# A two-layer encoder trunk on one core: inputs queued in source order behind early constant products, and a down-projection's late splits taken apart from their loads

## The chip, the cores and the metric

The kernel runs on one core of a Trainium2 chip. The metric is the device time of one execution in microseconds (us). Five engines work side by side, each through its own instructions in their order: TensorE (PE; its weight loads are shown as PEld), VectorE (DVE), ScalarE (ACT), GpSimd (POOL) and SyncE (SP). SP issues nearly all transfers; POOL issues those that add to their target.

## The reference

Input and output are 1024 frames x 1024 channels, float32. Two layers:

```
x = x + even_mixer(rms_norm(x))      # layer 0: stick-breaking attention (8 heads) beside a causal pooling mixer
x = x + conv_ffn(rms_norm(x))
x = x + odd_mixer(rms_norm(x))       # layer 1: gated linear attention, 4 heads
x = x + conv_ffn(rms_norm(x))

def conv_ffn(h, w_up, conv_w, conv_b, w_down):      # hidden width 2816
    u = h @ w_up
    conv = conv_b + sum(conv_w[j] * shifted(u, j) for j in range(3))
    a, g = split(conv, 2)
    return (silu(a) * g) @ w_down
```

## The kernel before, in words

Activations lie transposed, as eight tiles of 128 channels x 1024 frames (`x[0]` to `x[7]`). Each float32 operand of a matmul is split into a high part `hi` and a remainder `lo`: a cast on ACT, a subtraction on DVE. A product is three matmuls (hi x hi, hi x lo, lo x hi). So each weight and each activation has a chain of its own: load (SP), cast (ACT), subtraction (DVE), matmul (PE).

The order on TensorE is that of the source. The other engines are ordered by the scheduler when the kernel is built, within the data's dependences; `tc.manual_schedule` keeps the order of the source for the engines it names, and `tc.issue_after(ins)` puts what is written under it behind an instruction of the same engine. Each engine then runs its list strictly in order: one that waits holds up all behind it. A tile's buffer is reused when its readers are done.

**The start.** `prm` (norm gains and the like) and the eight tiles `xt` of the input are loaded; `Norm.add` splits each, scaled by its gain, into `h_hi` and `h_lo`, and adds its squares to `nacc`. Between the halves of the first tile stand the halves of the first query and key weights (`pq`, `pk`: the loads into `wraw` and `kg`, the casts, and the subtractions on POOL). `start_qk` multiplies the eight tiles with both weights in turn, 12 matmuls of 512 columns per tile, and then sums the squares with eight small f32 matmuls (`stats`, L286). Value weights (`in_wv`) follow, whose products (`values`) fill TensorE while the query and key chain runs. The parameters of the convolution (`prm[:, C_CONV:]`), the counts `cnt` and the pool weights `praw` are loaded early too.

**A down-projection** (`down`, once per layer) is one level of Strassen-Winograd: seven products, each of 11 steps `j`. Six are run in this order: P1, P5, P6, P3, P7, P4; a step is 12 matmuls into four banks. `prep(n, j)`, called three steps ahead (`LEAD`), fetches the step's right operand into `rb` (4 buffers; for P6 and P4 an accumulating transfer on POOL adds a second block), fetches its left operand into `rw` (4 buffers) where there is one, combines it on DVE (P5, P6, P3, P7), and splits both (`split_block`: two casts, two subtractions into `blk`). SP is on manual order here. The seventh product (P2) comes last, four rows `r` of 11 steps each. Its left operands are a row of weights as two loads, 512 KB into `wraw` (one buffer) and 192 KB into `r3` (one buffer; printed `r`), in rows of 512 bytes: `last_left`. Its right operands are the 11 blocks B21, 256 KB each: `last_right`, two to a tile `b21`. Both load and split at one call, the rows 0 and 1 within P6:

```
            if n == "P6" and j in (2, 6):
                rows[j // 4] = last_left(j // 4)
            k = NJ * (n == "P4") + j - 8
            if n in ("P7", "P4") and k % 2 == 0 and 0 <= k < NJ + 1:
                last_right(range(k, min(k + 2, NJ)))
```

In layer 0 two more loads follow P4's on SP, of the next mixer's key weights (`in_wok`), into `rb` buffers; their split is `kw`.

Of the kernel before, what the change touches and what calls it, by code (L numbers as in the profile page):

```python
# [12 lines left out]
F32 = mybir.dt.float32  # L13
R32 = mybir.dt.float32r
# [43 lines left out]
def trunk_kernel(  # L58
# [35 lines left out]
    def slot(dtype, name):  # L94
        return xpool.tile([P, T], dtype, tag="x", name=name)
# [15 lines left out]


    def load_split(src, pool=None, tags=("whi", "wlo", "wraw"), eng=None, nb=2, raw=None, parts=None,
                   fetched=None):
        srcs = src if isinstance(src, list) else [src]
        n = sum(a.free_size() for a in srcs)
        pool = pool or wpool
        if fetched is not None:
            raw = fetched
        elif raw is None:  # L120
            raw = (pool if len(tags) > 2 else wpool).tile([P, n], F32, tag=tags[2] if len(tags) > 2 else "wraw",
                                                      name="wraw", bufs=2 if "draw" in tags else 1)
# [13 lines left out]
        def part(cs):  # L136
            if fetched is None:
                fetch(cs)
            S.copy(hi[:, cs], raw[:, cs])  # L139
# [111 lines left out]
    class Norm:  # L251
        def __init__(self, gain_col, acc_tile, sq_tile, add_eng=None):
            self.col, self.acc_tile, self.sq_tile = gain_col, acc_tile, sq_tile
            self.h, self.add_eng, self.n = [None] * KT, add_eng, 0

        def add(self, x, parts=None, k=None):
# [11 lines left out]
            if self.n == 1:  # L268
                self.acc = self.acc_tile()
                S.activation(self.acc, x, AF.Square)  # L270
                return
            sq = self.sq_tile()
            S.activation(sq, x, AF.Square)
            (self.add_eng or (V if self.n == KT else G)).tensor_tensor(self.acc, self.acc, sq, op=ALU.add)

# [75 lines left out]
    ones = const.tile([P, P], F32, name="ones")  # L351
    G.memset(ones, 1.0)
    epsc = const.tile([P, 1], F32, name="epsc")
    G.memset(epsc, EPS)
# [49 lines left out]

    def values(half):
        wt = [load_split(wv[half, c], ep if half == 0 else None, ("ath", "atl") if half == 0 else ("whi", "wlo"))
              for c in range(2)]
        for pp in range(2):
# [784 lines left out]
    def split_block(src):  # L1193
        t = hpool.tile([P, T], R32, tag="h", name="blk")
        S.copy(t[:, 0:512], src)  # L1195
        V.tensor_sub(t[:, 512:T], src, t[:, 0:512].bitcast(F32))  # L1196
        return t

    def down(layer, blocks, ready, after, onward):
# [74 lines left out]

        def last_right(js):
            raw = hpool.tile([P, T], R32, tag="h", name="b21").bitcast(F32)
            for cs, j in zip(HALVES, js):
                nc.sync.dma_start(raw[:, cs], blocks[j]["B21"])
                hi = dn.tile([P, 512], R32, tag="ra", name="b21h", bufs=NJ)
                lo = dn.tile([P, 512], R32, tag="rs", name="b21l", bufs=NJ)  # L1280
                S.copy(hi, raw[:, cs])
                V.tensor_sub(lo, raw[:, cs], hi.bitcast(F32))
                b21.append((hi, lo))

        odd = wdn[layer].rearrange("(f two) p k -> two p f k", two=2)[1]

        def last_left(r):
            parts = []
            big = (hpool, ("wraw", "h", "h"), (1, 16, 16)) if r == KT // 2 - 1 else (wpool, ("wraw", "whi", "wlo"), (1, 2, 2))
            for k0, k1, (pool, tags, nb) in ((0, KT, big), (KT, NJ, (dn, ("r3", "r3h", "r3l"), (1, 2, 2)))):  # L1290
                raw, hi, lo = ((wpool if t == "wraw" else pool).tile([P, (k1 - k0) * P], d, tag=t, name=t, bufs=b)
                               for t, d, b in zip(tags, (F32, R32, R32), nb))
                nc.sync.dma_start(raw.rearrange("p (f k) -> p f k", k=P), odd[:, k0:k1, r * P:(r + 1) * P])
                S.copy(hi, raw)
                V.tensor_sub(lo, raw, hi.bitcast(F32))
# [49 lines left out]
        for r in range(half):  # L1345
# [389 lines left out]
```

## Time and profile before

| | |
|---|---|
| median of 3 runs | 2198.51 us (2197.76 to 2200.26) |
| profiled execution | 2199.35 us, span 2197.7 us |
| PE busy in it | 2150.8 us (98%) |
| DVE, ACT, POOL busy | 1664.8 (76%), 1093.1 (50%), 162.1 us (7%) |
| mean DMA traffic | 128 GB/s |
| longest idle of PE | 5.95 us, ahead of its first matmul |

The profiled execution's time lies 1.65 us above its span, which begins with the first and ends with the last recorded instruction. In the rows below, a start or a duration is in us; `[2.08 <-ACT blk L1195]` means that the engine was idle for 2.08 us before the instruction and that the ACT instruction writing `blk` at line 1195 ended that. L153, L155 and L157 are the three matmuls of `mm3`, L1266 those of a down-projection's step.

### The profile page before, as it was taken

To read this page: it belongs to the slowest core of one execution; us is meant where nothing else is said; L and a number is where in the kernel's file an instruction comes from. 1 tells how busy PE (TensorE), PEld (TensorE's weight loads), DVE (VectorE), ACT (ScalarE), POOL (GpSimd) and SP (SyncE) were. 2 spreads that over 40 slices of the span, in tenths; PEclk is the share of its full clock that TensorE was granted. 3 is DMA by queue.
4 is the path that set the end of the run, shared out by engine and by line. 5 is a ranking of instruction groups with operands and counts; after the bars stand their busy time and mean duration, and the time that the engine had idled before them with its cause. 6 is when DMAs were issued, how large, how long until landed. Compare 5 with 4: busy or idle time off the path is not lost.

```text
span 2197.7 us, 28082 instructions
## 1 busy us (share of the span) xinstructions
PE 2150.8 (98%) x10384; PEld 1767.0 (80%) x10384; DVE 1664.8 (76%) x2458; ACT 1093.1 (50%) x1705; POOL 162.1 (7%) x188
## 2 busy tenths in 40 slices
PE   8999989999999999999999999999999999999998
PEld 7889878888878888778887878787788888887776
DVE  5687688698989899777736655557898998987763
ACT  6666566464444444344546362637544444443441
POOL 2240120000000000010000000000000000000110
PEclk9999999999999999999999999999999999999999
DMA  4132332353444434987501111105343444449885
GB/s 152 49 107 87 94 112 94 119 130 106 130 119 126 124 116 124 350 216 233 169 21 40 38 49 38 49 30 145 105 124 116 123 122 120 124 157 327 222 239 157
DMA packets 126201, 280.31 MB, mean 128 GB/s; under 512 B 13408, under 2 KB 27360, under 8 KB 126064
## 3 DMA queue, kind: packets, MB, share of 16 engines
q1 hardware_dynamic: 112528, 251.25, 34.9%
q0 software_dynamic: 13536, 27.27, 7.0%
q8 instruction: 81, 1.33, 0.2%
q14 instruction: 56, 0.46, 0.1%
HBM read 208.21 MB, written 54.53 MB: 120 GB/s over the span
## 4 chain that ended last, share of the span: by engine, by line
PE 61%; DMA 15%; DVE 15%; issue 4%; ACT 4%; SPq 1%; POOL 0%; DVEq 0%; ACTq 0%; POOLq 0%
PE lin L936 10%; PE z L936 7%; PE lin L153 4%; PE lin L155 4%; PE lin L157 4%; DMA rb<-ut 4%; PE t L936 3%; PE d L936 3%; DMA rw<-in_wdn 3%; DVE blk L1196 2%; PE z L157 2%; PE z L153 2%; PE z L155 2%; DMA raw_g<-in_wup 2%; DMA wraw<-in_wup 2%
## 5 line engine op out<-in xcount | busy, mean ns | idle before, releaser
L1038 ACT ACTIVATE c<-u,prm 128x1024 f32<-128x1024 f32 x88 | 109.1, 1244 | 86.7 <-DVE u L964 79.1
L1266 PE MATMUL lin<-blk 128*128 128x512 f32 x396 | 118.6, 400 | 14.0 <-ACT blk L1195 8.6
L1196 DVE TENSOR_TENSOR blk<-rb,blk 128x512 fp32r<-128x512 f32 x124 | 85.1, 686 | 53.9 <-ACT blk L1195 53.4
L153 PE MATMUL lin<-h_hi,whi 128*128 128x512 f32 x288 | 114.2, 432 | 6.6 <-ACT whi L139 6.0
L1039 DVE SCALAR_TENSOR_TENSOR c<-u,prm,c 128x1023 f32<-128x1023 f32 x88 | 112.3, 1278 | 8.5 <-ACT c L1038 8.5
L1195 ACT CAST blk<-rb 128x512 fp32r<-128x512 f32 x124 | 76.6, 618 | 81.2 <-DMA rb<-ut 44.0
L936 PE MATMUL d<-T,a 128*128 128x512 f32 x480 | 115.4, 389 | 0.0
L1041 DVE SCALAR_TENSOR_TENSOR c<-u,prm,c 128x1022 f32<-128x1022 f32 x88 | 112.3, 1276 | 0.0
L1266 PE MATMUL t<-blk 128*128 128x512 f32 x396 | 112.0, 391 | 0.0
L1266 PE MATMUL d<-blk 128*128 128x512 f32 x396 | 111.9, 391 | 0.0
L1266 PE MATMUL z<-blk 128*128 128x512 f32 x396 | 111.6, 390 | 0.0
L964 DVE TENSOR_TENSOR u<-u,rstd_bc 128x512 f32<-128x512 f32 x160 | 107.8, 684 | 0.4
L936 PEld LDWEIGHTS d<-T,a 128*128 128x128 f32 x480 | 90.1, 188 | 18.7
L155 PE MATMUL lin<-h_lo,whi 128*128 128x512 f32 x288 | 104.4, 398 | 0.7 <-DVE h_lo L264 0.7
L1266 PEld LDWEIGHTS lin<-blk 128*128 128x128 f32 x396 | 73.0, 189 | 39.8 <-ACT blk L1195 13.2
L157 PE MATMUL lin<-h_hi,wlo 128*128 128x512 f32 x288 | 104.2, 398 | 0.0
L936 PE MATMUL z<-blk,s34h 128*128 128x512 f32 x320 | 101.3, 398 | 1.4 <-DVE u L995 1.4
L936 PE MATMUL z<-blk,s12h 128*128 128x512 f32 x320 | 100.9, 396 | 0.0
L936 PE MATMUL lin<-T,s34h 128*128 128x512 f32 x320 | 99.5, 392 | 0.8 <-ACT tm L986 0.8
L936 PE MATMUL t<-blk,whi 128*128 128x512 f32 x320 | 99.6, 392 | 0.0
L936 PE MATMUL lin<-blk,whi 128*128 128x512 f32 x320 | 99.5, 392 | 0.0
L936 PE MATMUL lin<-T,s12h 128*128 128x512 f32 x320 | 99.4, 391 | 0.0
(516 smaller groups left out, 6021.0 us busy)
## 6 DMA issues: line engine op xcount, KB each, us to landing
wraw<-in_wup SPq DMA_DIRECT2D x44, 512.0 KB, 3.7
rw<-in_wdn SPq DMA_DIRECT2D x88, 256.0 KB, 4.7
raw_g<-in_wup SPq DMA_DIRECT2D x40, 512.0 KB, 3.8
rb<-ut SPq DMA_DIRECT2D x66, 256.0 KB, 4.4
b<-c SPq DMA_DIRECT2D x22, 512.0 KB, 2.6
ut<-c SPq DMA_DIRECT2D x22, 512.0 KB, 3.8
s<-in_wup SPq DMA_DIRECT2D x40, 256.0 KB, 2.6
s<-s POOLq DMA_DIRECT2D x40, 256.0 KB, 4.4
```

What stands on the lines that cost most here:

```text
L153: PE.matmul(out[i], wh, ah[i], start=first, stop=False)
L155: PE.matmul(out[i], wh, al[i], start=False, stop=False)
L157: PE.matmul(out[i], wl, ah[i], start=False, stop=last)
L936: PE.matmul(ps, w, m, start=first and k == 0 and n == 0, stop=k == 3 and n == 2, skip_group_check=True)
L964: V.tensor_tensor(dst, dst, rstd_bc[:, cs], op=ALU.mult)
L1038: S.activation(c, u, AF.Identity, scale=pcol(b + 2), bias=pcol(b + 3))
L1039: V.scalar_tensor_tensor(c[:, 1:], u[:, :T - 1], pcol(b + 1), c[:, 1:], op0=ALU.mult, op1=ALU.add)
L1041: V.scalar_tensor_tensor(c[:, 2:], u[:, :T - 2], pcol(b), c[:, 2:], op0=ALU.mult, op1=ALU.add)
L1195: S.copy(t[:, 0:512], src)
L1196: V.tensor_sub(t[:, 512:T], src, t[:, 0:512].bitcast(F32))
L1266: PE.matmul(ps, l, m, start=first and j == 0 and i == 0, stop=j == NJ - 1 and i == 2, skip_group_check=True)
```

## The change

Four edits.

1. At the start, 24 f32 products of the constant tile `ones` with itself (`WARM`) go to TensorE ahead of all other matmuls; their result is not read.
2. The input loop puts SP on manual order. The loads of the input tiles stand ahead of all but the first halves of the query and key weights; the second halves follow the second and third tile; the value weights come behind the last tile, and conv parameters, counts and pool weights behind the value weights. The first halves' subtractions go to DVE. The second tile is split by halves too, and each addition to `nacc` stands one tile later.
3. `last_left` and `last_right` load at the call and return `later`, which splits. Row 0 is loaded at step 10 of P6 and split at step 3 of P3, row 1 at step 4 of P3 and split at step 9; the rows 2 and 3 load and split at one call, as before.
4. The B21 loads come two steps earlier (from step 6 of P7); their splits stay where they were. All moved splits are put behind the latest `split_block` (`behind_latest`).

```diff
+    warm = bank("d")
+    for _ in range(WARM):
+        PE.matmul(warm[:, 0:P], ones, ones, start=True, stop=True, skip_group_check=True)
...
+    queue = ExitStack()
+    queue.enter_context(tc.manual_schedule(engines={mybir.EngineType.SP}))
     for k in range(KT):
...
-            pq[1]()
-            pk[1]()
+            norm.first = split_ins[0]
         else:
             nc.sync.dma_start(xt, xT[k * P:(k + 1) * P, :])
-        norm.add(xt, HALVES if k == 0 else None)
-    nc.sync.dma_start(prm[:, C_CONV:], par[:, C_CONV:])
-    nc.sync.dma_start(cntc, cnt)
+            if k < 3:
+                (pq, pk)[k - 1][1]()
+        norm.add(xt, HALVES if k < 2 else None)
+    queue.close()
...
-            parts.extend(lambda cs=cs: part(cs) for cs in HALVES)
+            parts.extend(lambda cs=cs, e=e: part(cs, e) for cs, e in zip(HALVES, (V, eng)))
...
-    v0 = values(0)
+    v0 = values(0, value_weights(0))
+    inputs_in = split_ins[1]
+    with tc.issue_after(inputs_in):
+        nc.sync.dma_start(prm[:, C_CONV:], par[:, C_CONV:])
+        nc.sync.dma_start(cntc, cnt)
...
-            parts = []
+            raws = []
             for k0, k1, (pool, tags, nb) in ((0, KT, big), (KT, NJ, (dn, ("r3", "r3h", "r3l"), (1, 2, 2)))):
...
                 nc.sync.dma_start(raw.rearrange("p (f k) -> p f k", k=P), odd[:, k0:k1, r * P:(r + 1) * P])
-                S.copy(hi, raw)
-                V.tensor_sub(lo, raw, hi.bitcast(F32))
-                parts += [(hi[:, sl], lo[:, sl]) for sl in (slice(k * P, (k + 1) * P) for k in range(k1 - k0))]
-            return parts
+                raws.append((raw, pool, tags, nb))
+
+            def later():
+                parts = []
+                for raw, pool, tags, nb in raws:
+                    n = raw.free_size()
+                    hi, lo = (pool.tile([P, n], R32, tag=t, name=t, bufs=b) for t, b in zip(tags[1:], nb[1:]))
+                    S.copy(hi, raw)
+                    V.tensor_sub(lo, raw, hi.bitcast(F32))
...
+                rows[r] = parts
+            return later
...
+        ROWS, LATER = [("P6", 10), ("P3", 4)], [("P3", 3), ("P3", 9)]
...
-            if n == "P6" and j in (2, 6):
-                rows[j // 4] = last_left(j // 4)
-            k = NJ * (n == "P4") + j - 8
-            if n in ("P7", "P4") and k % 2 == 0 and 0 <= k < NJ + 1:
-                last_right(range(k, min(k + 2, NJ)))
+            if (n, j) in LATER:
+                with behind_latest():
+                    due.pop(0)()
+            if (n, j) in ROWS:
+                due.append(last_left(ROWS.index((n, j))))
+            k = NJ * (n == "P4") + j - 6
+            if n in ("P7", "P4") and k % 2 == 0 and 0 <= k < NJ + 3:
+                if due:
+                    with behind_latest():
+                        due.pop(0)()
+                if k < NJ + 1:
+                    due.append(last_right(range(k, min(k + 2, NJ))))
```

What SP issues first, before and then after (`xt` are input tiles, `wraw` and `kg` the query and key weights, `in_wv` the value weights; x7 is seven in a row):

```order
L347 DMA prm<-in_par 128x44
L391 DMA xt<-in_xT 128x512
L128 DMA wraw<-in_wqk 128x512
L391 DMA xt<-in_xT 128x512
L128 DMA kg<-in_wqk 128x512
L128 DMA wraw<-in_wqk 128x512
L128 DMA kg<-in_wqk 128x512
L398 DMA prm<-in_par 128x352
L399 DMA cntc<-in_cnt 128x64
L396 DMA xt<-in_xT 128x1024 x7
L570 DMA praw<-in_poolw 128x128 x2
L128 DMA wraw<-in_wv 128x1024
```

```order
L131 DMA kg<-in_wqk 128x512
L417 DMA xt<-in_xT 128x1024
L131 DMA wraw<-in_wqk 128x512
L417 DMA xt<-in_xT 128x1024
L131 DMA kg<-in_wqk 128x512
L417 DMA xt<-in_xT 128x1024 x5
L131 DMA wraw<-in_wv 128x1024 x2
L809 DMA prm<-in_par 128x352
L810 DMA cntc<-in_cnt 128x64
L596 DMA praw<-in_poolw 128x128 x2
```

The first five rows are the same in both; after them the second input tile now stands ahead of two half weights, the conv parameters and the counts.

What SP issues around the rows' loads in layer 0's down-projection, before (`rb<-ut` are right operands of P6) and then after (`rb<-b`, `rw` are P3's, from step 3 on):

```order
L1211 DMA rb<-ut_6253 128x512
L1293 DMA wraw<-in_wdn 128x8x128
L1293 DMA r_8168<-in_wdn 128x3x128
L1211 DMA rb<-ut_6514 128x512
L1211 DMA rb<-ut_6775 128x512
L1211 DMA rb<-ut_7036 128x512
L1211 DMA rb<-ut_7297 128x512
L1293 DMA wraw<-in_wdn 128x8x128
L1293 DMA r_8268<-in_wdn 128x3x128
L1211 DMA rb<-ut_7552 128x512
```

```order
L1338 DMA wraw<-in_wdn 128x8x128
L1338 DMA r_8373<-in_wdn 128x3x128
L1251 DMA rb<-b_5760 128x512
L1251 DMA rw<-in_wdn 128x512
L1251 DMA rb<-b_6021 128x512
L1251 DMA rw<-in_wdn 128x512
L1251 DMA rb<-b_6282 128x512
L1251 DMA rw<-in_wdn 128x512
L1251 DMA rb<-b_6543 128x512
L1251 DMA rw<-in_wdn 128x512
L1251 DMA rb<-b_6804 128x512
L1251 DMA rw<-in_wdn 128x512
```

Behind the last of these rows, step 7 of P3, stand the second row's two loads, and then step 8's `rb` and `rw`.

ACT at the end of P4 in layer 0, from step 9's left cast on, before and then after:

```order
L1195 CAST blk<-rw 128x512
L1195 CAST blk<-rb 128x512
L1195 CAST blk<-rw 128x512
L1195 CAST blk<-rb 128x512
L1281 CAST b21h<-b_9126 128x512
L1341 CAST kw<-rb 128x512 x2
```

```order
L1225 CAST blk<-rw 128x512
L1402 CAST kw<-rb 128x512 x2
L1225 CAST blk<-rb 128x512
L1225 CAST blk<-rw 128x512
L1225 CAST blk<-rb 128x512
L1325 CAST b21h<-b_9110 128x512
```

The two casts of the key weights have moved from behind P4's last split to between step 9's left and right casts.

More of the change, by code (lines that the diff above doesn't have):

```diff
@@ L41 @@
 FGROUP = 2
+WARM = 24
 C_MIXE = 0
@@ L253, in __init__ @@
             self.col, self.acc_tile, self.sq_tile = gain_col, acc_tile, sq_tile
-            self.h, self.add_eng, self.n = [None] * KT, add_eng, 0
+            self.h, self.add_eng, self.n, self.first = [None] * KT, add_eng, 0, None
         def add(self, x, parts=None, k=None):
@@ L269, in add @@
                 self.acc = self.acc_tile()
-                S.activation(self.acc, x, AF.Square)
+                with tc.issue_after(self.first) if self.first is not None else ExitStack():
+                    S.activation(self.acc, x, AF.Square)
                 return
@@ L273, in add, with add_up @@
             S.activation(sq, x, AF.Square)
-            (self.add_eng or (V if self.n == KT else G)).tensor_tensor(self.acc, self.acc, sq, op=ALU.add)
+            def add_up():
+                (self.add_eng or (V if self.n == KT else G)).tensor_tensor(self.acc, self.acc, sq, op=ALU.add)
+            if self.first is None:
+                add_up()
+                return
+            if self.n > 2:
+                with tc.issue_after(b.ins):
+                    self.due()
+            self.due = add_up
+            if self.n == KT:
+                add_up()
         def behind(self):
@@ L392, in trunk_kernel, with value_weights, values @@
                 p[0]()
-            pq[1]()
-            pk[1]()
+            norm.first = split_ins[0]
         else:
             nc.sync.dma_start(xt, xT[k * P:(k + 1) * P, :])
-        norm.add(xt, HALVES if k == 0 else None)
-    nc.sync.dma_start(prm[:, C_CONV:], par[:, C_CONV:])
-    nc.sync.dma_start(cntc, cnt)
+            if k < 3:
+                (pq, pk)[k - 1][1]()
+        norm.add(xt, HALVES if k < 2 else None)
+    queue.close()
     h = norm.h
     vt = [None] * NPAIR
-    def values(half):
-        wt = [load_split(wv[half, c], ep if half == 0 else None, ("ath", "atl") if half == 0 else ("whi", "wlo"))
-              for c in range(2)]
+    def value_weights(half):
+        return [load_split(wv[half, c], ep if half == 0 else None, ("ath", "atl") if half == 0 else ("whi", "wlo"))
+                for c in range(2)]
+    def values(half, wt=None):
+        wt = wt or value_weights(half)
         for pp in range(2):
@@ L778, in start_qk @@
         yield None
-    v0 = values(0)
+    v0 = values(0, value_weights(0))
+    inputs_in = split_ins[1]
+    with tc.issue_after(inputs_in):
+        nc.sync.dma_start(prm[:, C_CONV:], par[:, C_CONV:])
+        nc.sync.dma_start(cntc, cnt)
     fl = Filler()
@@ L1194, in split_block, with behind_latest @@
         t = hpool.tile([P, T], R32, tag="h", name="blk")
-        S.copy(t[:, 0:512], src)
-        V.tensor_sub(t[:, 512:T], src, t[:, 0:512].bitcast(F32))
-        return t
+        a = S.copy(t[:, 0:512], src)
+        b = V.tensor_sub(t[:, 512:T], src, t[:, 0:512].bitcast(F32))
+        latest[:] = a.ins, b.ins
+        return t
+    latest = []
+    def behind_latest():
+        st = ExitStack()
+        for ins in latest:
+            st.enter_context(tc.issue_after(ins))
+        return st
     def down(layer, blocks, ready, after, onward):
@@ L1278, in last_right @@
                 nc.sync.dma_start(raw[:, cs], blocks[j]["B21"])
[L1279 to L1283, printed above, removed]
+            def later():
+                for cs, j in zip(HALVES, js):
+                    hi = dn.tile([P, 512], R32, tag="ra", name="b21h", bufs=NJ)
+                    lo = dn.tile([P, 512], R32, tag="rs", name="b21l", bufs=NJ)
+                    S.copy(hi, raw[:, cs])
+                    V.tensor_sub(lo, raw[:, cs], hi.bitcast(F32))
+                    b21.append((hi, lo))
@@ L1285, in down @@
+            return later
         odd = wdn[layer].rearrange("(f two) p k -> two p f k", two=2)[1]
         def last_left(r):
-            parts = []
             big = (hpool, ("wraw", "h", "h"), (1, 16, 16)) if r == KT // 2 - 1 else (wpool, ("wraw", "whi", "wlo"), (1, 2, 2))
+            raws = []
             for k0, k1, (pool, tags, nb) in ((0, KT, big), (KT, NJ, (dn, ("r3", "r3h", "r3l"), (1, 2, 2)))):
-                raw, hi, lo = ((wpool if t == "wraw" else pool).tile([P, (k1 - k0) * P], d, tag=t, name=t, bufs=b)
-                               for t, d, b in zip(tags, (F32, R32, R32), nb))
+                raw = (wpool if tags[0] == "wraw" else pool).tile([P, (k1 - k0) * P], F32, tag=tags[0], name=tags[0], bufs=1)
@@ L1293, in last_left, with later @@
                 nc.sync.dma_start(raw.rearrange("p (f k) -> p f k", k=P), odd[:, k0:k1, r * P:(r + 1) * P])
-                S.copy(hi, raw)
-                V.tensor_sub(lo, raw, hi.bitcast(F32))
-                parts += [(hi[:, sl], lo[:, sl]) for sl in (slice(k * P, (k + 1) * P) for k in range(k1 - k0))]
-            return parts
+                raws.append((raw, pool, tags, nb))
+            def later():
+                parts = []
[4 more added lines that the diff above has]
+                    V.tensor_sub(lo, raw, hi.bitcast(F32))
+                    parts += [(hi[:, sl], lo[:, sl]) for sl in (slice(k * P, (k + 1) * P) for k in range(n // P))]
+                rows[r] = parts
@@ L1299, in down @@
+            return later
         LEAD = 3
@@ L1305, in down @@
         half = KT // 2
-        rows = {}
+        rows, due = {}, []
+        ROWS, LATER = [("P6", 10), ("P3", 4)], [("P3", 3), ("P3", 9)]
         for i, (n, j) in enumerate(order):
@@ L1350, in down @@
             if r + 2 < half:
-                rows[r + 2] = last_left(r + 2)
+                last_left(r + 2)()
             if r == 0:
```

9 lines of the change are left out of this document (5 added, 4 removed).

## The prediction

> **What bounds the kernel now.** I read the page first, then what TensorE waited for, then the down-projections stage by stage, then the single rows around each edit.
>
> ```profile
> PE 2150.8 (98%) x10384; PEld 1767.0 (80%) x10384; DVE 1664.8 (76%) x2458; ACT 1093.1 (50%) x1705; POOL 162.1 (7%) x188
> ```
>
> TensorE is the bound: 47 us of a 2197.7 us span are all that order can still win, besides half-clock time. Its longest sums of waiting (engine, instruction, releaser: us, times, longest):
>
> ```profile
> PE lin L1266 <- ACT blk L1195: 8.6, 10, 2.1
> PE lin L153 <- ACT whi L139: 6.0, 1, 6.0
> ```
>
> The first lies in the down-projections, the second is the kernel's start; the diff edits just these two places. A pass of a down-projection (P6, P3, P7, P4) is 11 steps of 12 matmuls. Busy time by pass, layer 0 and then layer 1:
>
> ```profile
> 943.80:980.80 37.00, 33.24 (x133) 25.70 (x132) 22.48 (x35) 17.11 (x30) 7.09 (x9) 0.95 0.93 225
> 980.80:1010.70 29.90, 29.90 (x133) 24.77 (x132) 26.10 (x43) 15.90 (x28) 0.00 (x0) 1.00 0.69 223
> 1010.70:1040.70 30.00, 30.00 (x134) 24.82 (x133) 19.34 (x32) 11.11 (x20) 3.77 (x5) 1.00 0.77 238
> 1040.70:1071.30 30.60, 30.38 (x134) 24.68 (x133) 23.42 (x38) 15.29 (x28) 5.74 (x7) 1.00 0.94 260
> 2030.40:2066.50 36.10, 31.63 (x133) 24.54 (x132) 21.25 (x33) 16.19 (x28) 6.92 (x8) 1.00 0.87 214
> 2066.50:2096.50 30.00, 30.00 (x134) 24.82 (x133) 26.31 (x44) 15.80 (x28) 0.00 (x0) 1.00 0.70 226
> ...
> 2126.40:2162.50 36.10, 32.24 (x134) 24.50 (x133) 24.45 (x39) 15.58 (x28) 6.05 (x7) 1.00 0.86 235
> ```
>
> The columns are window, sum, PE, PEld, DVE, ACT, POOL, clock, DMA share, GB/s. A pass that doesn't wait takes 29.9 us: 2.72 us a step, 0.227 us a matmul. P6 loses 7.1 and 6.2 us, P4 0.7 and 6.2. P3 and P7 (layer 1's P7 is left out) lose nothing, but DVE is busy 26 of 30 us in P3.
>
> **The late splits.** The rows of P6 in layer 0 that show the loss:
>
> ```profile
> 954.39 1.05 ACT L1294 CAST whi<-wraw 128x1024 fp32r<-128x1024 f32 x1 [1.59 <-DMA wraw<-in_wdn]
> 970.39 0.50 PE L1266 MATMUL lin<-blk 128*128 128x512 f32 x1 [2.08 <-ACT blk L1195]
> L1295 DVE TENSOR_TENSOR wlo<-wraw,whi 128x1024 fp32r<-128x1024 f32 x2 | 2.5, 1225 | 3.5 <-ACT whi L1294 3.5
> L1295 DVE TENSOR_TENSOR r3l<-r,r3h 128x384 fp32r<-128x384 f32 x2 | 1.1, 551 | 0.0
> ```
>
> ACT stands at a cast whose load has not landed, with the splits of P6 queued behind it. But TensorE's end is not set there alone. Call the splits the feed; its pace is read from the subtractions of step 0 of P6 and step 0 of P3, layer 0 and then layer 1:
>
> ```profile
> 941.22 0.69 DVE L1196 TENSOR_TENSOR blk<-rb,blk 128x512 fp32r<-128x512 f32 x1
> 976.35 0.68 DVE L1196 TENSOR_TENSOR blk<-rb,blk 128x512 fp32r<-128x512 f32 x1
> 2027.70 0.69 DVE L1196 TENSOR_TENSOR blk<-rb,blk 128x512 fp32r<-128x512 f32 x1
> 2064.31 0.68 DVE L1196 TENSOR_TENSOR blk<-rb,blk 128x512 fp32r<-128x512 f32 x1
> ```
>
> That is 35.1 and 36.6 us for 11 steps. The load also slows P6's own transfers. DMA landings from 932 to 945 us (first two lines, ahead of the load) and from 945 to 972:
>
> ```profile
> rb<-ut SPq DMA_DIRECT2D x5, 256.0 KB, 3.3
> rb<-b POOLq DMA_DIRECT2D x3, 256.0 KB, 4.2
> ...
> rb<-b POOLq DMA_DIRECT2D x8, 256.0 KB, 6.2
> rb<-ut SPq DMA_DIRECT2D x6, 256.0 KB, 5.5
> wraw<-in_wdn SPq DMA_DIRECT2D x2, 512.0 KB, 7.8
> ```
>
> One of four `rb` buffers is taken for load, accumulate, cast (1.05 for twice the size: 0.6) and subtraction (0.7): 3.3 + 4.2 + 1.3 = 8.8 us alone, 2.2 us a step, below TensorE's 2.72; 5.5 + 6.2 + 1.3 = 13.0 beside the load, 3.25 a step, above it. With the load and its casts gone P6 should not wait, and its feed takes 11 x 2.2 = 24 us at best; four x additions at its head (2.7 us of DVE) make it 27. The feed is ahead by 8.1 and 9.6 us at P3. What it pays back:
>
> - The second row's load stands on SP behind step 7 of P3, and its buffer is free only after the first row's subtraction, which DVE runs behind step 6's splits; step 8's `rb` and `rw` wait behind it on SP. Step 8's splits come 3.4 us (two x additions and the first row's two subtractions) + L + 2.0 (subtraction, cast, subtraction) after step 6's, where DVE needs 2 x 2.4 now (26.1 us for 11 steps). L is a landing behind 704 KB: between 3.3 (the `rb` row) and 7.8 (the `wraw` row), nearer the first since nothing accumulates there: 5. So 5.6 lost. The steps behind, landed meanwhile, win back some 1.5; the first row's load slows the loads of steps 3 and 4 by about 1. P3 pays 5.1, bounds 3.4 and 7.9. The casts on ACT are covered (16 us of 30 busy).
> - The second row's subtractions (1.23 + 0.55 = 1.8 us) go to the head of P7, where DVE is busy 19 of 30 us: I take half, 0.9.
> - Two of the eleven B21 loads that run beside P4's own now go ahead of them: 5% of 11 x (768 + 256) KB, and of P4's 31 to 36 us some 1 us gained (0 to 1.5). The B21 splits stay in place.
>
> Layer 0: 8.1 - 5.1 - 0.9 + 1.0 = 3.1, bounds -1.6 and 6.2. Layer 1: 4.6 by the same sum; P6's 6.2 is all there is to win, so I take 4.0 between 0 and 6.2. In both layers most of the stall that P6 loses is late again in P4, where TensorE then waits for `rb`: only what the feed gains is kept. SP's queue is otherwise unmoved, POOL's accumulates keep their order.
>
> **The key weights at the end of P4, layer 0 only.** The scheduler now puts both `kw` casts ahead of step 9's `rb` cast on ACT. The rows before (SP's issue, step 9's cast, the second `kw` cast):
>
> ```profile
> 1058.36 5.16 SPq L1211 DMA_DIRECT2D rb<-in_wok  x2
> 1064.41 0.62 ACT L1195 CAST blk<-rb 128x512 fp32r<-128x512 f32 x1 [0.42 <-DMA rb<-ut]
> 1067.81 0.62 ACT L1341 CAST kw<-rb 128x512 fp32r<-128x512 f32 x1 [0.37 <-DMA rb<-in_wok]
> ```
>
> The second load waits for step 8's buffer, so its landing moves with step 8. Step 9's cast goes from 1064.4 to 1067.8 + 0.5, 3.9 us later, and ends at 1068.9. P4 ends at 1071.3 in the table, so step 9 began two steps earlier, at 1065.9: TensorE waits 3.0. A wait of that length has a second price:
>
> ```profile
> 968.90:972.30 3.40, 1.69 (x6) 1.18 (x7) 1.76 (x3) 2.15 (x5) 0.82 (x1) 1.00 1.02 253
> 972.30:975.70 3.40, 3.40 (x10) 2.64 (x9) 3.09 (x5) 2.20 (x5) 0.00 (x0) 0.50 0.91 275
> 2054.30:2057.70 3.40, 1.64 (x8) 1.02 (x6) 1.22 (x1) 1.65 (x3) 0.86 (x1) 1.00 1.09 254
> 2057.70:2061.10 3.40, 3.11 (x13) 2.37 (x14) 3.05 (x6) 2.09 (x5) 0.00 (x0) 1.00 0.97 176
> ```
>
> After a stretch of 3.4 us with PE half idle the clock was 0.50 for the next 3.4 us (1.7 us lost); after another as idle, in layer 1, it was not. At 3.0 us idle I take the dip at 8 in 10: 1.4. Together -4.4, bounds -4.7 and 0. The Trainium skill ("TensorE: Matmul & The Clock Gate", Part 1) has it that the clock is gated after at least one idle window of about 3.4 us; by that there would be no dip and the term would be -3.0. The row at 972 differs, after only 2.1 us of idling, and the row decides.
>
> **The start.**
>
> ```profile
> 0.95 0.21 POOL L352 MEMSET ones<- 128x128 f32 x1
> 5.95 1.58 PE L153 MATMUL lin<-h_hi,whi 128*128 128x512 f32 x2 [5.95 <-ACT whi L139]
> 8.46 1.06 PE L157 MATMUL lin<-h_hi,wlo 128*128 128x512 f32 x2
> 9.31 0.82 PE L153 MATMUL t<-h_hi,whi 128*128 128x512 f32 x2
> 9.97 0.62 PE L155 MATMUL t<-h_lo,whi 128*128 128x512 f32 x2
> 10.46 1.15 ACT L263 ACTIVATE h_hi<-xt,prm 128x1024 fp32r<-128x1024 f32 x1 [1.27 <-DMA xt<-in_xT]
> 31.86 1.84 PE L286 MATMUL d<-ones,nacc 128*128 128x2 f32 x16
> 10.00:20.00 10.00, 8.66 (x37) 6.55 (x36) 8.36 (x8) 9.54 (x10) 1.98 (x2) 1.00 0.92 363
> ```
>
> The first tile runs at half clock (8.46 to 9.31: 0.43 us a matmul; from 9.97 on 0.23); the eight tiles end at 31.86. The 24 products of constants are 48 records (the code's 8 f32 matmuls at L286 are 16) of 1.84/16 = 0.115 us, 0.23 at half clock, and can start at 1.2, when `ones` is set. If half a busy stretch of 3.4 us is enough, as above, the clock rises 1.7 to 5.1 us after that; in the middle, at 4.7, 7.5 of the 24 are done, the other 16.5 take 3.8: they end at 8.5 (7.6 to 9.4). That is later than 5.95, but all 96 real matmuls then run at 0.23: 8.5 + 22.1 = 30.6, gain 1.2. Bounds 0.4 and 1.6, since the data ends it: the second tile, with 0.72 MB less ahead at 363 GB/s, lands 2.0 us sooner and is split at 10.6, 0.7 before its turn. Splits on DVE (0.7 us) in place of POOL (1.3) are covered; the second value load waits for the first one's split, as before, and is used only behind the stats matmuls; conv parameters, counts and pool weights go behind it, and no work of the first 40 us reads them but one cast of pool weights, on ACT, which has gaps there.
>
> By the same section of the Trainium skill, a whole free-running window has to be busy before the clock rises: 3.4 to 6.8 us after the start, so that the products would end between 8.4 and 10.1 and the term be -0.3 to 1.3. The rise before 9.97 for a start at 5.95 fits both, and no other row here tells them apart.
>
> **Sum.** 1.2 + 3.1 - 4.4 + 4.0 = 3.9 us. The profiled execution took 2199.35 (span 2197.7, the rest lies around it): 2195.4. It stands 0.8 above the median of 2198.51, so for a median I say 2194.6.
>
> **Rivals.**
> - The `kw` casts cost nothing, because the feed is ahead at P4's end or the load lands sooner. For: P4 of layer 0 loses only 0.7 now. Against: there TensorE no longer stands 7 us in P6, and the feed is only 3 us sooner. 3.9 + 4.4 = 8.3: 2190.2.
> - All that P6 loses (13.3) is kept and nothing comes back. For: P3 and P7 lose nothing now, with DMA at 0.69 to 0.77. Against: P4 of layer 1 waits already. 14.5: 2184.
> - Slower: the second row's load holds SP for longer than the feed has in hand. Two steps of TensorE are 5.4 us, so it stalls at step 8 of P3 for L + 3.4 + 2.0 - 5.4 = L less what is in hand at step 6. At step 0 of P3 that is 980.8 - 977.0 = 3.8 now, 4.8 by the sum, and more at step 6; it decides when L passes that. With L = 7.8 and 2 in hand (1.5 at step 0 of P3 in layer 1 now) TensorE idles 5.8 with a dip of 1.7, 15.0 in both layers: 15.0 + 4.4 - 13.3 - 1.2 = 4.9 more, 2203.4.
> - It does little: the feed gains nothing, `kw` waits less, the start stays: 2198.
>
> **Chances.** Forecast case (2192 to 2198) 0.42; `kw` free 0.24; all kept 0.09; SP held 0.13; little 0.12. 0.2% is 4.4 us, about what a measurement of this kernel can tell: faster means below 2194.1. Faster 0.24 + 0.09 + 0.17 of the forecast case = 0.50; slower is over half of the SP rival, 0.08; within 0.42. The range leaves out the case of all kept and the slower half of the SP rival: 2187.5 to 2201.
>
> **What would show it.** First real matmul near 8.5 and the stats matmuls near 30.6; P6 near 30 us in both layers; a wait on SP ahead of P3's second `wraw`, and DVE waiting for `rw` of step 8; P4 longer in layer 0, with ACT waiting on `in_wok` and TensorE idle some 3 us, PEclk below 1 after it. Wrong if P3 shows PE idle, if P4 of layer 0 stays at 30.6, or if `kw` doesn't wait.

## The result, and the profile after

| | before | after |
|---|---|---|
| median of 7 runs | 2197.76 us (2193.97 to 2202.03) | 2210.36 us (2203.23 to 2215.10) |
| ratio after / before, with 95% interval | | 1.0052 (1.0039 to 1.0065): some 11 us slower |
| profiled execution, span | 2199.35, 2197.7 | 2210.36, 2208.7 |

The forecast was 2194.6 in a range of 2187.5 to 2201: the sign was wrong. Busy time of the engines after:

```profile
PE 2158.1 (98%) x10432; PEld 1773.3 (80%) x10432; DVE 1667.5 (75%) x2461; ACT 1091.5 (49%) x1706; POOL 160.5 (7%) x186
```

To find where the time went, the two traces' matmuls were matched one by one in TensorE's order; the table gives how much later (plus) or earlier (minus) each kernel's TensorE starts the same matmul than the profiled execution of before, at marks on the clock of before (us). The pass named at a mark is the one that ends there; differences along a row are what each stretch cost. A row is one execution, and not always a typical one: those of e1 and e14 took 4.6 and 6.0 us more than the medians of their kernels. A half-clock stretch, below, is one of 3.4 us in which the granted clock of TensorE was 0.50.

| kernel | 62, start | 423, attention | 940, P5 | 980, P6 | 1010, P3 | 1040, P7 | 1073, P4 | 1519 | 1570 | 2029, P5 | 2066, P6 | 2096, P3 | 2161, P4 |
|---|---|---|---|---|---|---|---|---|---|---|---|---|---|
| after | -0.9 | -5.1 | -4.7 | -10.3 | -4.0 | -4.0 | +4.6 | +4.9 | +10.6 | +9.6 | +4.7 | +9.6 | +11.0 |
| start alone (e1) | -0.2 | -4.6 | -5.8 | -3.5 | -3.5 | -3.5 | +2.2 | +1.3 | +7.9 | +6.9 | +5.2 | +5.2 | +7.4 |
| down alone (e2) | +0.8 | -2.2 | -2.5 | -7.0 | -0.8 | -0.8 | +5.7 | +5.1 | +5.1 | +4.3 | +0.4 | +6.0 | +6.7 |
| rows alone (e3) | +1.3 | -0.8 | -1.9 | -7.5 | -2.2 | -2.2 | +0.8 | +0.8 | +0.8 | +1.0 | -2.5 | +1.9 | -0.7 |
| B21 alone (e4) | +0.3 | -2.8 | -3.3 | -6.3 | -6.3 | -6.3 | +4.7 | +4.2 | +4.2 | +3.0 | +4.9 | +4.9 | +5.8 |
| order of inputs alone (e5) | +1.9 | 0.0 | -0.1 | -1.9 | -1.9 | -1.9 | +2.7 | +2.1 | +2.1 | +2.3 | +0.6 | +0.6 | -0.6 |
| products alone (e6) | +0.2 | -4.6 | -4.4 | -1.9 | -1.5 | -1.5 | +0.8 | +0.8 | +8.3 | +7.1 | +7.4 | +7.4 | +6.6 |
| late second row (e7) | +0.9 | -0.9 | -2.2 | -8.3 | -8.3 | -8.3 | -1.6 | -1.7 | -1.7 | -1.9 | -6.6 | -6.6 | -3.8 |
| 64 products (e14) | +8.3 | +10.2 | +9.4 | +8.2 | +8.2 | +8.2 | +13.8 | +13.7 | +13.7 | +13.1 | +12.1 | +12.1 | +12.3 |

Between 62 and 423 nothing was changed, and the kernels still differ there, from 4.8 us won (e6) to 1.9 lost (e14): half-clock stretches fall there or not (three between 180 and 275 in before, none in after). Only stretches that were edited, or that differ in all kernels with an edit, are read.

**The start** came out at the times that were said (starts and busy time of TensorE, after):

```profile
1.21 7.15 PE L372 MATMUL d<-ones 128*128 128x128 f32 x48 [1.21 <-POOL ones L368]
8.11 0.71 PE L156 MATMUL lin<-h_hi,whi 128*128 128x512 f32 x2
30.83 1.84 PE L302 MATMUL d<-ones,nacc 128*128 128x2 f32 x16
```

The first real matmuls are later than before (5.95) and at full clock, and the sums of squares stand 1.0 us earlier than before (31.86). The experiments put that gain down to the order of the inputs and not to the products: the sums stand at 31.90 with the products alone (e6), at 31.32 and 31.11 with the order alone (e5, e13), and between 31.86 and 33.02 in the eight kernels whose start is the old one.

**The passes**, in the same columns as in the prediction (P6, P3 and P4, layer 0 and then layer 1):

```profile
939.10:970.60 31.50, 30.82 (x134) 24.68 (x133) 17.35 (x28) 13.20 (x24) 7.00 (x9) 1.00 0.93 220
970.60:1006.70 36.10, 32.05 (x133) 25.81 (x133) 26.62 (x43) 16.84 (x30) 0.00 (x0) 0.95 0.62 201
...
1036.60:1075.90 39.30, 32.99 (x134) 25.70 (x133) 25.22 (x41) 16.94 (x30) 6.05 (x7) 0.96 0.78 204
2040.00:2071.20 31.20, 30.77 (x134) 24.64 (x133) 17.50 (x29) 13.20 (x24) 6.92 (x8) 1.00 0.92 220
2071.20:2106.10 34.90, 32.12 (x134) 25.86 (x133) 25.80 (x42) 16.11 (x28) 0.00 (x0) 0.95 0.65 207
...
2136.10:2174.20 38.10, 33.74 (x137) 26.26 (x136) 24.74 (x40) 14.80 (x27) 6.05 (x7) 0.96 0.80 212
```

P6 fell from 37.0 and 36.1 to 31.5 and 31.2. P3, which took 29.9 and 30.0, takes 36.1 and 34.9; P4 of layer 0 takes 39.3 in place of 30.6. The clock column shows a half-clock stretch in P3 and in P4 of both layers. Of the waits of SP's queue between 960 and 1075, in layer 0, these matter here, after and then before (us, times, longest):

```profile
SPq L1338 <- DVE wlo L1347: 9.4, 1, 9.4
SPq L1319 <- DVE b21l L1326: 5.5, 1, 5.5
```

```profile
SPq L1278 <- DVE b21l L1282: 1.7, 2, 1.5
```

The first line is the wait in P3 that the prediction named: the second row's load (L1338) stands on SP until the first row's subtraction (`wlo`) has freed `wraw`. The second is new and was not forecast: a B21 load (L1319) stands 5.5 us for the subtraction of an earlier B21 tile. Both stop TensorE (first two rows: step 8 of P3; third row: step 5 of P4). The fourth row, step 9 of P4, is the wait behind the key weights:

```profile
995.70 0.50 PE L1306 MATMUL lin<-blk 128*128 128x512 f32 x1 [3.14 <-ACT blk L1225]
997.11 0.73 PE L1306 MATMUL lin<-blk 128*128 128x512 f32 x2 [0.91 <-DVE blk L1226]
1054.32 0.49 PE L1306 MATMUL lin<-blk 128*128 128x512 f32 x1 [2.78 <-ACT blk L1225]
1069.90 0.49 PE L1306 MATMUL lin<-blk 128*128 128x512 f32 x1 [2.30 <-ACT blk L1225]
```

In the timeline the B21 wait reads so (SP's issues, the end of the subtraction that it waited for, and the cast behind the late load):

```profile
1034.03 0.43 SPq L1251 DMA_DIRECT2D rw<-in_wdn  x1
1040.00 0.83 SPq L1319 DMA_DIRECT2D b<-b  x2
1041.24 0.32 SPq L1251 DMA_DIRECT2D rb<-ut  x1
```

```profile
1038.69 1.28 DVE L1326 TENSOR_TENSOR b21l<-b,b21h 128x512 fp32r<-128x512 f32 x2
```

```profile
1053.65 0.62 ACT L1225 CAST blk<-rb 128x512 fp32r<-128x512 f32 x1 [6.42 <-DMA rb<-ut]
```

SP stands from 1034.5 to 1040.0, until the subtraction (1038.69 + 1.28) ends. Only then does it issue step 5's `rb` at 1041.24, which lands and is accumulated to by 1053.6. A raw B21 tile (`b21`) is one of the 16 buffers of the tag `h` that all `blk` splits use in turn. Loaded two steps earlier and split where it always was, it holds its buffer longer than the ring takes to come round, so that SP has to wait for the subtraction which frees it.

**The middle** shows a loss in code that no edit touched: between 1519 and 1570, at the end of the odd mixer, after falls 5.7 us behind. There ACT writes the squares `nsq` in turn, and POOL's accumulating transfers add them to `nacc`, each after the one before it has landed. The third and the sixth of the squares, before and then after:

```profile
1524.37 1.04 ACT L332 ACTIVATE nsq<-x 128x1024 f32<-128x1024 f32 x1
...
1540.01 1.06 ACT L332 ACTIVATE nsq<-x 128x1024 f32<-128x1024 f32 x1 [1.75 <-DVE T L918]
```

```profile
1531.45 1.06 ACT L348 ACTIVATE nsq<-x 128x1024 f32<-128x1024 f32 x1 [1.97 <-DMA nacc<-nsq]
...
1549.71 1.06 ACT L348 ACTIVATE nsq<-x 128x1024 f32<-128x1024 f32 x1 [4.16 <-DMA nacc<-nsq]
```

The first two squares stand 5.0 us later in after, as all else does there; the third stands 7.1 later and the sixth 9.7. TensorE in the end waits 2.0 us ahead of the sums of squares, with a half-clock stretch behind it (clock 0.50 from 1564.3 to 1567.7); before it did not wait at that place. Before, and then after:

```profile
1552.86 1.84 PE L286 MATMUL t<-ones,nsq 128*128 128x2 f32 x16
...
1561.76 1.95 PE L302 MATMUL t<-ones,nsq 128*128 128x2 f32 x16 [1.97 <-DVE nsq L357]
```

The transfers of the same 9 us, from the first `xs` load on, before (1515 to 1524) and then after (1520 to 1529); `xs` and the accumulates are issued by SP and POOL (KB each, median us to landing), and q8 is a queue that carries instructions (packets, MB, share):

```profile
xs<-x SPq DMA_DIRECT2D x4, 512.0 KB, 4.2
nacc<-nsq POOLq DMA_DIRECT2D x1, 512.0 KB, 4.6
```

```profile
q8 instruction: 1, 0.02, 1.1%
xs<-x SPq DMA_DIRECT2D x4, 512.0 KB, 6.0
nacc<-nsq POOLq DMA_DIRECT2D x1, 512.0 KB, 7.2
```

Before has no q8 transfer in its 9 us. The only thing added in after is one 16 KB transfer of instructions, and the accumulate takes 2.6 us longer to land. The three accumulates behind it take 5.2, 5.8 and 5.7 us (5.0, 5.0 and 4.6 before), now issued within 0.5 us of an `xs` load; how one small transfer slows the large ones is not shown by the traces. Which engine's instructions these are, the whole page of after tells:

```profile
q8 instruction: 82, 1.34, 0.3%
```

1.34 MB over TensorE's 2 x 10432 instructions (matmuls and weight loads) is 64 bytes each, which fits q8 carrying TensorE's code, 256 instructions to a transfer. The 24 constant products are 48 + 48 instructions: they move every later transfer of code ahead by 96 instructions, some 11 us at 0.227 us for two. In before the transfer falls at 1528.8, in after at 1523.2, which on the clock of before is 1518.3 (transfers from 1528 to 1530 in before, from 1523 to 1525 in after):

```profile
q8 instruction: 1, 0.02, 2.8%
```

```profile
q8 instruction: 1, 0.02, 5.1%
```

### The profile page after: what moved, and what is told of

The parts are those of the page before. It is cut to its first block, busy times and chain, and to the rows that moved or that the text cites. A ratio compares the mean times of both kernels' runs of the same rounds, so it can differ in the third digit from the quotient of the medians.

```text
span 2208.7 us, 28152 instructions
## 1 busy us (share of the span) xinstructions
PE 2158.1 (98%) x10432; PEld 1773.3 (80%) x10432; DVE 1667.5 (75%) x2461; ACT 1091.5 (49%) x1706; POOL 160.5 (7%) x186
## 3 DMA queue, kind: packets, MB, share of 16 engines
q1 hardware_dynamic: 112528, 251.25, 34.9%
q8 instruction: 82, 1.34, 0.3%
```

## The experiments

Two theories stood against one another. The queue theory: the loss is made by two waits on SP in the down-projections. Its rival, or companion: the start costs it, in the middle. Each ratio below is to the kernel before, timed beside it on the same chip, with its 95% interval; 0.001 is 2.2 us.

**e1, edits 1 and 2 alone; e2, edits 3 and 4 alone.**

> Edits 1 and 2 alone (the constant products and the order of the inputs); the down-projections are as before. The trace after lies 0.9 us ahead of the trace before at 90 us, 5.1 at 270 (before has three half-clock stretches between 180 and 275 us that after lacks) and 4.9 behind it again between 1520 and 1565, where nothing was changed. Queue theory (the loss is made in the down-projections by two waits on SP): 0.9 us faster for sure, up to 5 if the half-clock stretches went away because of the start: 2193 to 2198 against 2198, and 1520 to 1565 not late. Rival (the start shifts the whole kernel against its accumulating transfers and costs some 5 us in the middle): 2198 to 2203, with TensorE idle ahead of the sums of squares near 1560.

> Edits 3 and 4 alone (rows split apart from their loads, B21 loads two steps earlier); the start is as before. Queue theory: all of the loss is here: P6 wins 5.7 in both layers, P3 loses 6.3 and 5.1, P4 loses 9.0 (2.3 of it the key weights) and 1.4: +5.4 us, and not less than +2: 2201 to 2210. Rival (the loss is the start's or the middle's): 2195 to 2200.

Measured: e1 1.0013 (0.9999 to 1.0027), e2 1.0039 (1.0024 to 1.0054). Together 1.0052, which is all of after. In its profiled execution e1 loses 6.6 us in the middle, e2 nothing there (table), so the queue theory is not the whole. By its time alone e1 cannot be told from before; e6, below, is what shows the start's price in time.

**e3, edit 3 alone; e4, edit 4 alone.**

```diff
# e3, against after (start as before)
-            k = NJ * (n == "P4") + j - 6
...
+            k = NJ * (n == "P4") + j - 8
+            if n in ("P7", "P4") and k % 2 == 0 and 0 <= k < NJ + 1:
+                last_right(range(k, min(k + 2, NJ)))()
# e4, against after (start as before)
-            if (n, j) in LATER:
...
+            if n == "P6" and j in (2, 6):
+                last_left(j // 4)()
```

> Edit 3 alone: the rows' loads and splits as after, B21 loads and splits at one call as before. Queue theory: P6 wins 11.4 in both layers together, and P3 pays 11.4 because the second row's load holds SP for 9 us behind the first row's subtraction: -3 to +3 us, 2195 to 2201, with PE idle in step 8 of P3 (3 to 4 us and a half-clock stretch) and P4 of layer 0 without the 2.8 us wait at step 5 and without the key weights' wait. Rival (the rows alone carry the loss): 2203 to 2212. Rival of the prediction (P3 pays only 5): 2189 to 2193.

> Edit 4 alone: B21 loads two steps ahead of their splits, rows loaded and split within P6 as before. Queue theory: SP waits some 5 us in both layers for the subtraction of an earlier B21 tile (its buffer), with P4's own loads queued behind it, so TensorE waits 0.8 and 2.8 us at steps 3 and 5 of P4, and 2.3 for the key weights: +4 to +10 us, 2202 to 2208. Rival (earlier B21 loads help or are free, as the prediction took them): 2195 to 2199, or up to 2202 if the key weights alone cost 2.3 to 4.4.

Measured: e3 0.9997 (0.9986 to 1.0007), e4 1.0044 (1.0030 to 1.0059). P3 and P4 of layer 0 in e3:

```profile
973.30:1008.50 35.20, 32.10 (x133) 25.85 (x133) 26.01 (x43) 16.20 (x28) 0.00 (x0) 0.95 0.65 206
...
1038.40:1071.40 33.00, 31.18 (x131) 23.94 (x130) 23.00 (x38) 15.48 (x28) 6.05 (x7) 1.00 0.92 260
```

The rows' edit wins 5.6 and 3.5 us in the two P6, and P3 takes back 5.3 and 4.4. Edit 4 makes the loss in the down-projections. Its wait on SP and P4 of layer 0:

```profile
SPq L1289 <- DVE b21l L1296: 5.3, 1, 5.3
```

```profile
1035.10:1076.70 41.60, 34.42 (x134) 26.65 (x133) 26.07 (x42) 18.01 (x31) 6.04 (x7) 0.92 0.75 194
```

**e5, the order of inputs without products; e6, the products alone.**

> The start's new order of inputs without the constant products (edit 2 alone). Both kernels with the products lose 5.7 and 6.6 us near 1520 to 1565, where a 16 KB transfer of instructions falls at 1519.9 and 1523.2, among the loads and the first accumulate of the norm's sums; in the three traces without the products it falls elsewhere (1528.8 in before) and nothing is lost. Theory (the 96 instructions of the products move where TensorE's code is fetched): the instruction transfer is back near 1529, no idle ahead of the sums of squares near 1556; the first tile runs at half clock again: 2195 to 2199. Rival (the order of inputs, or the drift of transfers, makes the loss in the middle): 2200 to 2205 with the same idle of some 2 us.

> Before with the 24 constant products alone (edit 1). Theory of the moved code fetch: 5 to 6 us lost near 1520 to 1565 as in the other two kernels with the products, 1.2 at most won at the start: 2201 to 2206. Rival (chance, or the order of inputs): no loss there, 2195 to 2199.

Measured: e5 0.9994 (0.9984 to 1.0005), e6 1.0034 (1.0021 to 1.0048). The products alone lose 7.5 us in the middle, the order nothing. e1, which has both, came out 4.6 us below e6, more than the order alone wins (1.3); how much of that is the spread of the intervals, or of executions that do not lose in the middle, is open. e6's transfers over the same 9 us:

```profile
q8 instruction: 1, 0.02, 0.9%
xs<-x SPq DMA_DIRECT2D x4, 512.0 KB, 5.9
nacc<-nsq POOLq DMA_DIRECT2D x1, 512.0 KB, 7.1
```

**e7, the second row's load where SP need not wait; e8, B21 loaded and split at one call, both two steps earlier.**

```diff
# e7, against e3
-        ROWS, LATER = [("P6", 10), ("P3", 4)], [("P3", 3), ("P3", 9)]
+        ROWS, LATER = [("P6", 10), ("P3", 9)], [("P3", 3), ("P7", 3)]
# e8, against before
-            k = NJ * (n == "P4") + j - 8
+            k = NJ * (n == "P4") + j - 6
```

> Edit 3 with the second row's load issued at step 9 of P3 in place of step 4, and split at step 3 of P7; B21 and start as before. Queue theory: by then the first row's subtraction has long been done, SP does not wait for it, and P3 no longer pays its 9.5 (4.4 in layer 1, 5.3 in layer 0 in the trace with edit 3 alone), while P6 keeps its 5.6 and 3.5: 2188 to 2192. Rival (the load itself, not SP's wait, slows P3, and would slow P7 as well): 2195 to 2199. Rival (what P6 wins is late again in P4, which waits for its accumulated operands): 2194 to 2198, with longer waits in P4.

> Before with loads and splits of B21 both two steps earlier (edit 4 without its taking apart). The key weights' casts stand ahead of step 9's last splits here too, so their wait of 2.3 us, with a half-clock stretch at worst, stays. Queue theory (what costs is the buffer that a loaded B21 tile holds until its late split): no wait of 5 us on SP for a B21 subtraction, no 2.9 us wait at step 5 of P4: 2199 to 2203. Rival (the earlier transfers themselves push P4's operands back): 2205 to 2211 with the waits of steps 3 and 5 as in edit 4.

Measured: e7 0.9990 (0.9980 to 1.0001), e8 1.0018 (1.0005 to 1.0031). P3 and P4 of layer 0 in e7:

```profile
972.50:1002.40 29.90, 29.90 (x134) 24.76 (x133) 25.14 (x41) 13.91 (x25) 0.00 (x0) 1.00 0.75 249
...
1033.90:1069.50 35.60, 32.72 (x132) 24.16 (x133) 26.80 (x44) 18.17 (x34) 6.90 (x8) 1.00 0.95 264
```

P3 loses nothing, and neither does P7 up to its last matmul, though the load now runs beside it (the table has -8.3 at 1010 and at 1040). So the load alone is free there, and what P3 paid was SP's wait. But P4 then takes 35.6, and with a wait of 1.3 us ahead of its first matmul it gives back 6.7 and 2.8 us of the two layers' gain: the rival that P6's win is late again in P4 held. In e8 the long wait for a B21 subtraction is gone,

```profile
SPq L1278 <- DVE b21l L1282: 0.3, 1, 0.3
```

and so is more than half of e4's loss: 1.0044 to 1.0018. That is the price of taking the splits apart from the loads, 5.7 us, give or take 4 by the two intervals. The profiled execution of e8, which took 6.2 us more than the median of e8, shows less of it: P4 of layer 0 still takes 39.2 us (41.6 in e4), though no wait of 2.9 us stands at step 5 any more. What is left are 1.91 us at step 3 and 2.45 us at step 9, behind the key weights, each with a half-clock stretch:

```profile
1042.20:1081.40 39.20, 34.38 (x134) 26.91 (x133) 24.65 (x40) 16.76 (x30) 6.91 (x8) 0.91 0.79 213
```

**e9, six products of 512 columns for the 24 of 128; e10, e8 with the key weights' splits kept last; e11, e7 and e10 together.**

```diff
# e9, against before
+    warm = bank("d")
+    wide = etile("pw", F32, 528)[:, 0:512]
+    G.memset(wide, 1.0)
+    for _ in range(6):
+        PE.matmul(warm, ones, wide, start=True, stop=True, skip_group_check=True)
# e10, against e8: the key weights' casts and subtractions
+                with behind_latest():
+                    S.copy(hi, t)
+                    V.tensor_sub(lo, t, hi.bitcast(F32))
```

> Before with six constant products of 512 columns in place of 24 of 128 columns (ones times a tile of ones that POOL sets): about the same work for TensorE in 24 instructions, not 96. Theory of the moved code fetch: the 16 KB transfer that falls at 1518.6 (on the clock of before) with the 24 products falls 8 us later, near 1526, past the first loads and the first accumulate of the norm's sums, so that the 7.5 us lost near 1520 to 1565 do not occur: 2195 to 2200. Rival (any constant products at the start cost it, by the clock or by the time shift): 2203 to 2208 with the same 2 us idle ahead of the sums of squares.

> The kernel with loads and splits of B21 both two steps earlier, and the key weights' splits kept behind P4's last splits. Against that kernel (2203.1): if the key weights' wait is what is left of its loss, 2.4 us and a half-clock stretch of 1.7 in part of the runs go: 2199 to 2201, with no wait on in_wok ahead of P4's end. If the earlier transfers are what is left: 2202 to 2205.

> Row loads at step 10 of P6 and step 9 of P3 (splits at step 3 of P3 and of P7), B21 loaded and split two steps earlier, key weights' splits behind P4's last. With the late second row alone P6 and P3 won 6.7 and 4.7 us in the two layers, and P4 gave back 6.7 and 2.7, since it waits for its accumulated operands. If B21's transfers within P4 are what holds those operands, moving two of eleven ahead gives some back: 2192 to 2196. If P4's pace is set by its own loads and accumulates: 2195 to 2199.

Measured: e9 0.9991 (0.9981 to 1.0002), e10 0.9999 (0.9987 to 1.0011), e11 0.9996 (0.9985 to 1.0007). e9 has no loss in the middle (0.0 us from 1519 to 1570). Against e8, e10 shows what the key weights cost: 0.0019, 4.2 us, give or take 4; P4 of layer 0 falls from 39.2 to 34.1:

```profile
1037.80:1071.90 34.10, 30.84 (x133) 24.62 (x132) 24.83 (x41) 16.27 (x29) 6.75 (x8) 1.00 0.91 247
```

The earlier transfers themselves cost nothing that can be told from e10's time. e11 is no better than e7: moving two of B21's eleven loads ahead does not free P4's operands. That P4's own loads and accumulates set its pace is then the likely reason; no run varies them, so it is not shown.

**e12 and e13, the change mended (late second row, B21 as before) with six wide products and with none; e14, 64 products of 128 columns on the kernel before.**

> The changed kernel with three mends: six products of 512 columns in place of 24, the second row's load at step 9 of P3 (split at step 3 of P7), B21 loaded and split at one call as before. If the parts add (inputs' order 0.9994, wide products 0.9991, late second row 0.9990): 0.9975, 5.5 us faster than before, 2191 to 2195. If the start's parts do not add, since the data ends it: 2194 to 2197.

> The same without any constant products. If the parts add: 0.9984, 2193 to 2197. It lies some 2 us above the one with six products if these are worth what they gave alone, and level with it if the order of the inputs had given that already.

> Before with 64 constant products of 128 columns: 256 more instructions for TensorE, which at 64 bytes each are one whole 16 KB transfer, so that the transfers of code fall where they fall in before. The products end 80 records of 0.115 us later than 24 do, at 17.2, so the start costs 7 to 8 us. Theory of the moved code fetch: nothing is lost near 1520 to 1565, the transfer falls near 1529 on the clock of before: 2203 to 2208. Rival (the products themselves, or the shift in time, cost the 7 us in the middle): 2210 to 2216 with TensorE idle 2 us ahead of the sums of squares.

Measured: e12 1.0020 (1.0008 to 1.0032), e13 0.9998 (0.9988 to 1.0008), e14 1.0034 (1.0021 to 1.0048), 2205.62. e14 settles the middle: 40 products more than e6, and yet from 1519 to 1570 nothing is lost; what it loses, 7.8 us by its median, it has lost by 62 us (8.3 in the table). In its 9 us no code is fetched, and the transfers take what they took in before:

```profile
xs<-x SPq DMA_DIRECT2D x4, 512.0 KB, 4.0
nacc<-nsq POOLq DMA_DIRECT2D x1, 512.0 KB, 4.7
```

Where the code transfer stands fits the count of instructions in every trace. It starts this long behind the first `xs` load: 13.7 us in before and 13.5 to 14.2 in the nine others without products; 3.2 to 3.5 with the 24 products (after, e1, e6); 9.9 and 9.6 with the six wide ones, 24 instructions (e9, e12); 14.0 with the 64 (e14). Only the three kernels with 3.2 to 3.5 lose anything between 1519 and 1570 (5.7, 6.6 and 7.5 us; 0.2 at most in the others).

The mends did not add up: neither e12 nor e13 came out as expected, and no version is faster than before beyond its interval. In the profiles of e9 and e12 TensorE stands 2.9 and 3.6 us at 41 us, behind a DVE instruction (`kl<-ident,rstd_tok`) that took 3.05 us in place of 1.70, and runs 6.8 us at half clock from there. The traces show what stands beside it: there POOL's subtraction of `wlo` starts 0.4 us ahead of it and takes 2.4 us, while in before and in e13 the DVE instruction starts 0.7 us ahead of POOL's, takes 1.7, and POOL's takes 3.2. Why the two change places, and why e12 loses 0.0020 in time where e9 loses nothing, is open.

## Why the prediction was wrong

Three steps of the sum failed: the start's term, which counted nothing beyond the start; the B21 term, which had the wrong sign; and the feed's gain, which was taken some three times too large in layer 0. The signs that the prediction named for itself split: "P3 shows PE idle" came, while P4 of layer 0 did get longer and `kw` did wait.

- **Start, +1.2 us: right in time at the start, and wrong as a sum.** First matmul 8.11 (8.5 said), sums of squares at 30.83 (30.6 said), though by e5 and e6 it was the order and not the products that gained it. What failed is the step that left the products' price at those 40 us. They move TensorE's code transfers, and one fell among the loads and accumulates of a serial chain 1500 us later: 7.5 us in e6, 5.7 in after.
- **The slower rival, SP held by the second row's load: it came, at the size of the forecast's own term.** P3 pays 6.2 and 5.0 (36.1 and 34.9 less 29.9); 5.1 was said, bounds 3.4 to 7.9. It was given 0.13 because the feed was believed to be well ahead: 4.8 us at P3 in layer 0 by the prediction's sum, 0.8 in after (P3 begins at 970.60, and the subtraction ends at 969.09 + 0.68, below).
- **P6 near 30 us: nearly right (31.5, 31.2). The feed's gain behind it was the mis-sized term.** I took 27 us for 11 steps from landings of 3.3 and 4.2 us ahead of the load. Without any load of a row, P6 of after shows (DMA issues from 940 to 963, median us to landing):

```profile
rb<-b POOLq DMA_DIRECT2D x8, 256.0 KB, 5.2
rb<-ut SPq DMA_DIRECT2D x6, 256.0 KB, 4.2
```

  4.2 + 5.2 + 1.3 = 10.7, 2.7 us a step: TensorE's own pace. The subtractions of step 0 of P6 and of P3 stand 32.3 us apart (35.1 before):

```profile
936.79 0.69 DVE L1226 TENSOR_TENSOR blk<-rb,blk 128x512 fp32r<-128x512 f32 x1 [0.31 <-ACT blk L1225]
969.09 0.68 DVE L1226 TENSOR_TENSOR blk<-rb,blk 128x512 fp32r<-128x512 f32 x1
```

  So the feed gained 2.8, not 8.1, and 5.1 in layer 1 (36.6 to 31.5), not 9.6. With these gains the prediction's own sum for the rows is -3.2 and -0.9: nothing is won, and e3 measured 0.9997.
- **B21, +1.0 us: the wrong sign, and the largest miss in the down-projections.** "The B21 splits stay in place" was read as a step that costs nothing; with the loads moved and the splits not, each tile holds a buffer of the ring for longer, and SP stands for it with P4's operands queued behind. "SP's queue is otherwise unmoved" was true of its order and not of its waits. Price: 5.7 us (e4 less e8, give or take 4).
- **Key weights, -4.4 us: the wait was right, and the size is near.** ACT stood 4.0 us for the second load (3.9 said) and TensorE 2.3 (3.0 said). The half-clock stretch, put at 1.4, did not follow in this execution; in e4 and e8 it did, after 2.25 and 2.45 us. e10 against e8 gives 4.2. The second row is step 9's cast, which stands behind it:

```profile
1068.71 0.62 ACT L1402 CAST kw<-rb 128x512 fp32r<-128x512 f32 x1 [4.01 <-DMA rb<-in_wok]
1069.23 0.61 ACT L1225 CAST blk<-rb 128x512 fp32r<-128x512 f32 x1
```

  It comes with edit 4 and not with edit 3: in e3 these casts stand last, and in e8, where B21 is loaded and split two steps earlier, they stand ahead.
- **The half-clock stretch after an idle of some 2 to 4 us: right as a risk.** After the two idles in P3 (two stretches of 3.4 us, then the next):

```profile
990.80:994.20 3.40, 1.76 (x8) 1.13 (x6) 0.49 (x1) 0.00 (x0) 0.00 (x0) 1.00 1.02 304
994.20:997.60 3.40, 0.99 (x3) 0.64 (x4) 2.64 (x6) 2.17 (x4) 0.00 (x0) 1.00 0.72 278
997.60:1001.00 3.40, 3.40 (x10) 2.65 (x9) 3.40 (x7) 2.38 (x5) 0.00 (x0) 0.52 0.71 224
```

  TensorE was never idle for a whole 3.4 us, and the clock fell all the same, as in the prediction's row at 972 and against the rule of the Trainium skill ("TensorE: Matmul & The Clock Gate", Part 1) quoted there. The 2.30 us ahead of 1069.90 brought none, and 2.25 us at the same step in e4 did (clock 0.50 from 1068.6): the length of the idle time alone does not decide it.

Together, by ratios: products and order 2.9, edit 4 9.7 (taking apart 5.7, key weights 4.2), edit 3 nothing: 12.6 us, against the 11.4 measured, a difference well within the intervals. The forecast's sum was 3.9 faster.

## What to carry to other kernels

When a load is moved ahead of its use and its reader is not, the buffer is held for the difference: look for what asks for that buffer next and which queue waits there, even if no instruction of that queue was moved. A gain in one pass is kept only if the supply behind it is faster than the engine; measure that pace where the disturbance is absent for a whole pass, not over its first few steps. And added instructions have a price away from where they stand: they shift an engine's code transfers against everything that follows.

## What the runs showed of the hardware

- TensorE's code arrives by DMA in transfers of 16 KB (256 instructions of 64 bytes; 82 in the 2208.7 us of after, one in some 27 us), each busy for 0.9 to 1.8 us there. One that fell among four 512 KB loads and an accumulate raised the accumulate from 4.6 to 7.2 us, and a chain of such accumulates then lost 5.7 to 7.5 us. The Trainium skill ("Runtime: NRT & Kernel Launch", Instruction fetch mechanics) has the refill in 16 KiB blocks of 256 instructions, which these runs agree with, and calls the cost of crossing a block mostly hidden; here three kernels (after, e1, e6) paid for it, and the ones in which the transfer fell elsewhere did not.
- 96 instructions at the start decide where it falls (3.2 to 3.5 us behind the first `xs` load in place of 13.7); 256 (e14) put it back where it was (14.0).
- Where two elementwise instructions of 128x1024 overlapped near 40 us, one on DVE and one on POOL, the one that started second took longer: DVE 3.05 us in e9 (1.70 in before), POOL 3.2 in before (2.4 in e9).
